# Column sums for the shift and scale vectors of a two-block kernel: transposes with a sum on VectorE, or matmuls with a column of ones

## The chip, the cores and the metric

One core of a Trainium2 chip runs the whole program in one launch. The metric is the device time of an execution in microseconds (us). TensorE (PE) multiplies, VectorE (DVE) and ScalarE (ACT) work on its outputs, GpSimd (POOL) has a small part, and SyncE (SP) issues the transfers.

## What is computed

Two stacks of transformer-like blocks over 256 tokens of width 1024, all in float32. Each of the twelve sublayers normalises its input and shifts and scales it by vectors that come from a conditioning vector:

```python
mod = cond @ ada_w[l] + ada_b[l]                  # 1024 -> 9 * 1024
sh1, sc1, g1, sh2, sc2, g2, sh3, sc3, g3 = jnp.split(mod, N_MOD, axis=-1)
h = modulate(x, norm_ffn1[l], sh1, sc1)           # rms_norm(x, gain) * (1 + scale) + shift
x = x + 0.5 * (1.0 + g1)[:, None] * swiglu(h, ffn1_w1[l], ffn1_w3[l], ffn1_w2[l])
```

The sublayers are feed-forward networks, two mixers with a gated delta rule and latent attention, one state-space mixer, and one pooling mixer. Two sublayers of the second stack also run over a second sequence, with a conditioning vector of its own. What the change touches is `cond @ ada_w` for the shift and scale vectors alone.

## The kernel before, in words

Weights stream through a ring of seven 128x1024 tiles (`raw`). ACT rounds each to a short form (`hi`, L354), DVE takes the rest (`lo`, L355), and TensorE multiplies three times (L360 to L362); some layers multiply whole float32 tiles instead (L386, L412). Outputs of these products stand in the PSUM tag `mm`, four tiles; all other TensorE outputs stand in the tag `ps`, four tiles of 128x512.

The modulation vectors are made in the background, a step at a time between the units of weights (`tick`). `Mods.sums` takes one vector of 1024: for each of eight blocks of 128 input features it loads a 128x1024 piece of `ada_w` into a ring of two tiles (`ad`), and adds it, scaled by the conditioning value of its partition, to a tile `acc` (one buffer): ACT starts it (L537), DVE adds the seven others (L541). Where two conditioning vectors are served, the second has two 128x512 tiles (`pg`) of its own. Then the 128 partitions of `acc` have to be summed.

For gates this sum is wanted as a row on every partition, and `rows` multiplies by a 128x128 block of ones (L559). For shift and scale it is wanted as eight columns of 128, feature by partition, and `cols` (L546) makes it: for each half of `acc`, four 128x128 transposes by TensorE into a `ps` tile (`T4`, L248), and one sum along the free axis by DVE (L551) of 128x512 to 128x4; then the bias is added (L552). `scale` multiplies by the gain afterwards (L586). Ten sublayers take shift and scale this way, two of them for two conditioning vectors, so `cols` runs 24 times; the first sublayer has its own path (`early`), and the pooling mixer uses `rows`.

The order on each engine is not written by hand: a planner orders the instructions at build time by their place in the program, by free tiles and by its own costs; only the weights' loads, `hi` and `lo` are held in sequence (`in_order`). Each engine then runs its list in that order.

A sum by a column of ones is already in use elsewhere, for the norms of queries and keys (L1065): a 128x128 block is the weight, one column of ones moves, and one column of PSUM is written, 16 times in each of four passes through that code.

Of the kernel before, what the change touches and what calls it, by code (L numbers as in the profile page):

```python
# [14 lines left out]
ALU = mybir.AluOpType  # L15
AX = mybir.AxisListType
# [7 lines left out]
KD = D // P  # L24
# [51 lines left out]
def block_kernel(ctx, tc, A, out, stop=None, skip=()):  # L76
    nc = tc.nc
    V, G, T = nc.vector, nc.gpsimd, nc.tensor
# [27 lines left out]
    def nm(s):  # L106
        names[0] += 1
        return f"{s}_{names[0]}"

    def ps():  # L110
        return psp.tile([P, 512], F32, tag="ps", name=nm("ps"))
# [7 lines left out]
    def small(n, dt=F32, tag="sm", bufs=None):  # L119
        return smp.tile([P, n], dt, tag=f"{tag}{n}", name=nm(tag), **({"bufs": bufs} if bufs else {}))  # L120
# [8 lines left out]
    def C(n):  # L129
        a, w = CI[n]  # L130
        return con[:, a:a + w]

    ident, ones = C("ident"), C("ones")
# [39 lines left out]
    gain, adab = {}, {}  # L173
# [24 lines left out]
    def h4(ap):  # L198
        return ap.rearrange("p (h d) -> p h d", d=P)
# [12 lines left out]
    SL = [slice(h * P, (h + 1) * P) for h in range(4)]  # L212
# [33 lines left out]
    def T4(o, src):  # L246
        for sl in SL[0:src.shape[1] // P]:
            T.transpose(o[:, sl], src[:, sl], ident)  # L248
# [256 lines left out]
    class Mods:  # L505
# [38 lines left out]
            yield  # L544

        def cols(self, i, v, tag):  # L546
            o = small(KD, tag=tag, bufs=8)
            for h in range(2):
                q = ps()
                T4(q, self.acc[i][h])  # L550
                V.tensor_reduce(out=o[:, h * 4:h * 4 + 4], in_=h4(q), op=ALU.add, axis=AX.X)  # L551
            V.tensor_add(o, o, adab[self.b, self.l][:, v * KD:(v + 1) * KD])  # L552
            return o

        def rows(self, i, o, mul, add):
# [1564 lines left out]
```

## Time and profile before

| | |
|---|---|
| median of 3 runs | 3086.33 us (3085.15 to 3090.08) |
| the profiled execution, its own time | 3087.46 us |
| its span, first to last instruction | 3085.7 us |
| busy: PE, DVE, ACT, POOL | 2950.2, 2214.3, 1339.0, 162.1 us |
| mean granted TensorE clock | 0.98 |
| moved from and to memory | 606 MB read, 4 MB written |

Busy times are sums over the span, and they are averages over stages with different limits. A stretch of the span has to be read by itself: which engine has no gap in it, and which wait ends last there. The granted clock is given as a share of 2.4 GHz; it has two levels, 1.00 and 0.50. Matmuls overlap, so the mean duration of one is longer than the distance from one to the next; what a group occupies is read from the chain of waits, which gives each piece the time that passed in it. The weight loads (PEld) run beside the matmuls.

### The profile page before, as it was taken

The numbers are of one execution on the slowest core, as the hardware profiler recorded it, in microseconds if no ns is written. First come the engines' busy times: TensorE is split into PE (matmuls) and PEld (weight loads), VectorE is DVE, ScalarE is ACT, GpSimd is POOL, SyncE is SP. The second block draws the span as 40 slices with busy tenths as digits, with TensorE's granted clock in tenths as the row PEclk, the third lists the DMA queues.
The fourth block names the chain that finished last, engine by engine and source line by source line (L and its number), as shares of the span: only waits on it lengthen the run. The fifth ranks groups of instructions, "written<-read, shape, count | busy, mean of one in ns | idle before, by whom it ended". The sixth has DMA issues, their size and how long they took to land.

```text
span 3085.7 us, 44006 instructions
## 1 busy us (share of the span) xinstructions
PE 2950.2 (96%) x16707; PEld 2444.7 (79%) x16707; DVE 2214.3 (72%) x3980; ACT 1339.0 (43%) x2096; POOL 162.1 (5%) x148
## 2 busy tenths in 40 slices
PE   7999999999998999999999999999989999999898
PEld 4988889875575898978876589899865799897697
DVE  6799988665388657887665385675789976878754
ACT  4554454322244445443322354544544644443443
POOL 1000000100002000000100000000043000001000
PEclk9999999999999999999999999999999999999899
DMA  8788886323464857894223475686534487788563
GB/s 280 251 287 292 259 296 208 89 73 106 153 203 170 264 185 229 290 318 131 81 78 109 139 245 183 197 295 194 172 89 130 145 284 233 232 292 296 157 185 129
DMA packets 288921, 613.25 MB, mean 199 GB/s; under 512 B 29480, under 2 KB 75702, under 8 KB 288709
## 3 DMA queue, kind: packets, MB, share of 16 engines
q1 hardware_dynamic: 288709, 610.44, 61.0%
q8 instruction: 131, 2.15, 0.3%
q14 instruction: 81, 0.66, 0.1%
HBM read 606.16 MB, written 4.20 MB: 198 GB/s over the span
## 4 chain that ended last, share of the span: by engine, by line
PE 68%; DVE 17%; DMA 8%; issue 4%; ACT 3%; POOL 1%; SPq 0%; DVEq 0%; ACTq 0%; POOLq 0%
PE mm L360 16%; PE mm L361 15%; PE mm L362 15%; PE mm L386 9%; DMA ad<-ada_w 6%; PE mm L412 4%; DVE acc L541 3%; PE ps L248 2%; DVE lo L355 2%; DVE pg L541 1%; PE ps L1172 1%; PE ps L1165 1%; PE ps L559 1%; DVE pg L1519 1%; DVE pg L1522 1%
## 5 line engine op out<-in xcount | busy, mean ns | idle before, releaser
L354 ACT CAST hi<-raw 128x1024 fp32r<-128x1024 f32 (+1 forms) x587 | 611.1, 1044 | 790.9 <-PE mm L361 308.0
L355 DVE TENSOR_TENSOR lo<-raw,hi 128x1024 fp32r<-128x1024 f32 (+1 forms) x587 | 709.0, 1218 | 293.8 <-ACT hi L354 280.9
L360 PE MATMUL mm<-hTh,lo 128*128 128x256 f32 x2448 | 702.1, 287 | 20.6 <-DVE lo L355 11.7
L361 PE MATMUL mm<-hTh,hi 128*128 128x256 f32 x2448 | 694.4, 284 | 0.0
L362 PE MATMUL mm<-hTl,hi 128*128 128x256 f32 x2448 | 693.9, 284 | 0.1
L360 PEld LDWEIGHTS mm<-hTh,lo 128*128 128x128 f32 x2448 | 470.2, 192 | 27.9 <-DVE lo L355 9.0
L361 PEld LDWEIGHTS mm<-hTh,hi 128*128 128x128 f32 x2448 | 470.7, 192 | 2.3 <-issue 1.2
L362 PEld LDWEIGHTS mm<-hTl,hi 128*128 128x128 f32 x2448 | 470.4, 192 | 0.3 <-DVE hTl L726 0.3
L541 DVE SCALAR_TENSOR_TENSOR acc<-ad,cond,acc 128x1024 f32<-128x1024 f32 x238 | 305.2, 1282 | 82.0 <-DMA ad<-ada_w 80.1
L360 PE MATMUL mm<-hi,pg 128*128 128x512 f32 (+1 forms) x716 | 281.1, 393 | 0.0
L361 PE MATMUL mm<-hi,pg 128*128 128x512 f32 (+1 forms) x716 | 277.5, 388 | 0.0
L362 PE MATMUL mm<-lo,pg 128*128 128x512 f32 (+1 forms) x716 | 275.6, 389 | 0.9 <-DVE lo L355 0.9
L386 PE MATMUL mm<-raw,hTw 128*128 128x512 f32 x448 | 212.1, 604 | 0.0
L412 PE MATMUL mm<-hTw,raw 128*128 128x256 f32 x896 | 204.5, 382 | 1.3 <-ACT pg L1514 1.3
L360 PE MATMUL mm<-hi,hTl 128*128 128x512 f32 (+1 forms) x424 | 174.1, 411 | 22.9 <-DVE hTl L726 14.5
L412 PEld LDWEIGHTS mm<-hTw,raw 128*128 128x128 f32 x896 | 168.7, 191 | 28.5 <-issue 5.0
L386 PE MATMUL mm<-raw,pg 128*128 128x512 f32 (+1 forms) x416 | 179.0, 574 | 1.2 <-ACT pg L1180 1.2
L361 PE MATMUL mm<-hi,hTh 128*128 128x512 f32 (+1 forms) x424 | 167.1, 395 | 0.0
L362 PE MATMUL mm<-lo,hTh 128*128 128x512 f32 (+1 forms) x424 | 166.7, 394 | 0.4 <-DVE lo L355 0.4
L362 PEld LDWEIGHTS mm<-lo,pg 128*128 128x128 f32 x716 | 134.4, 188 | 29.3 <-DVE lo L355 1.6
L360 PEld LDWEIGHTS mm<-hi,pg 128*128 128x128 f32 x716 | 134.7, 188 | 28.6 <-issue 2.0
L361 PEld LDWEIGHTS mm<-hi,pg 128*128 128x128 f32 x716 | 134.7, 188 | 27.7 <-issue 1.0
(433 smaller groups left out, 4355.8 us busy)
## 6 DMA issues: line engine op xcount, KB each, us to landing
ad<-ada_w SPq DMA_DIRECT2D x272, 512.0 KB
raw<-ffn_w SPq DMA_DIRECT2D x264, 512.0 KB
raw<-ffn_w_gate SPq DMA_DIRECT2D x110, 512.0 KB
raw<-ffn_w_up SPq DMA_DIRECT2D x110, 512.0 KB
raw<-ffn_w_down SPq DMA_DIRECT2D x110, 512.0 KB
raw<-w_in SPq DMA_DIRECT2D x104, 512.0 KB
raw<-ssd_w_in SPq DMA_DIRECT2D x60, 512.0 KB
raw<-w_branch_a SPq DMA_DIRECT2D x16, 512.0 KB
```

The costliest lines, as they stand in the source:

```text
L248: T.transpose(o[:, sl], src[:, sl], ident)
L354: in_order("hi", ACT.copy(hi[:, 0:m], raw[:, 0:m]))
L355: in_order(lane, eng.tensor_sub(lo[:, 0:m], raw[:, 0:m], hi[:, 0:m]))
L360: T.matmul(o, sl, mh, start=first, stop=False)
L361: T.matmul(o, sh, mh, start=False, stop=False)
L362: T.matmul(o, sh, ml, start=False, stop=last)
L386: T.matmul(d[c0 // 512][:, 0:min(cw, c0 + 512) - c0], sf, wt[c0 // 512], start=k == 0, stop=k == kt - 1)
L412: T.matmul(acc[m][:, 0:S], wt[0][:, SL[m]], hT.whole[:, k, :], start=k == 0, stop=k == KD - 1)
L541: after_edge(V.scalar_tensor_tensor(out=o, in0=w, scalar=sc, in1=o, op0=ALU.mult, op1=ALU.add))
L559: T.matmul(q, ones, self.acc[i][h], start=True, stop=True)
L1165: T.matmul(blk(y[:, H2[h]]), M[t][:, sl], odd(Ub[t][:, sl]), start=True, stop=True)
L1172: T.matmul(z[:, H2[h]], Tb[t][:, sl], Y[t][:, H2[h]], start=True, stop=True)
```

## The change

For the eight columns there are now eight matmuls. Each takes one 128x128 block of `acc` as its weight and one column of ones as its moving operand, and writes one column of a single `ps` tile. The bias is added straight from that tile. The two DVE sums, the second `ps` tile and the transposes are gone. Nothing else is edited.

```diff
         def cols(self, i, v, tag):
-            o = small(KD, tag=tag, bufs=8)
-            for h in range(2):
-                q = ps()
-                T4(q, self.acc[i][h])
-                V.tensor_reduce(out=o[:, h * 4:h * 4 + 4], in_=h4(q), op=ALU.add, axis=AX.X)
-            V.tensor_add(o, o, adab[self.b, self.l][:, v * KD:(v + 1) * KD])
+            o, q = small(KD, tag=tag, bufs=8), ps()
+            for k in range(KD):
+                T.matmul(q[:, k:k + 1], self.acc[i][k // 4][:, SL[k % 4]], ones[:, 0:1], start=True, stop=True)
+            V.tensor_add(o, q[:, 0:KD], adab[self.b, self.l][:, v * KD:(v + 1) * KD])
             return o
```

## Rows read from the trace of the kernel before

**Rows 1.** The page, busy time of each engine over the span.
```profile
PE 2950.2 (96%) x16707; PEld 2444.7 (79%) x16707; DVE 2214.3 (72%) x3980; ACT 1339.0 (43%) x2096; POOL 162.1 (5%) x148
```
**Rows 2.** TensorE's order of time, L248 on `acc`: start, us, count, idle before.
```profile
158.23 1.09 PE L248 MATMUL ps<-con,acc 128*128 128x128 f32 x8 [0.75 <-DVE acc L541]
...
2829.95 1.09 PE L248 MATMUL ps<-con,acc 128*128 128x128 f32 x8 [0.69 <-DVE acc L541]
```
**Rows 3.** Stretches: length, busy PE, PEld, DVE, ACT, POOL (records), clock, DMA, GB/s.
```profile
160.00:180.00 20.00, 16.63 (x124) 16.24 (x123) 19.65 (x28) 7.72 (x9) 0.00 (x0) 0.91 0.76 248
180.00:200.00 20.00, 17.29 (x117) 15.34 (x116) 19.27 (x26) 9.02 (x13) 0.00 (x0) 1.00 0.83 277
...
300.00:320.00 20.00, 15.89 (x122) 14.99 (x121) 20.00 (x25) 7.32 (x10) 0.00 (x0) 0.97 0.82 253
```
**Rows 4.** The same view around two of the later bursts.
```profile
1240.00:1260.00 20.00, 20.00 (x171) 20.00 (x170) 14.75 (x19) 10.84 (x16) 0.00 (x0) 1.00 0.86 300
...
2040.00:2060.00 20.00, 20.00 (x171) 20.00 (x170) 15.15 (x20) 10.34 (x15) 0.00 (x0) 1.00 0.80 276
```
**Rows 5.** Chain of waits: start, us, piece, instructions merged; a transpose burst, then L1065.
```profile
2047.40 0.87 PE ps L248 x8
```
**Rows 6.** Chain of waits over the whole span: one burst at L1065.
```profile
547.15 1.68 PE ps L1065 x16
```
**Rows 7.** Groups by form: records | busy us, mean ns | idle before.
```profile
L248 PE MATMUL ps<-con,acc 128*128 128x128 f32 x160 | 21.4, 274 | 4.7 <-DVE acc L541 4.7
...
L1065 PE MATMUL ps<-con,pg 128*128 128x1 f32 x128 | 17.7, 264 | 0.0
...
L1065 PEld LDWEIGHTS ps<-con,pg 128*128 128x128 f32 x128 | 18.9, 222 | 1.5 <-ACT pg L1061 0.5 <-issue 0.5
```
**Rows 8.** Groups by form on DVE.
```profile
L551 DVE TENSOR_REDUCE msh<-ps 128x4 f32<-128x512 f32 x24 | 15.6, 685 | 4.4 <-PE ps L248 4.4
...
L552 DVE TENSOR_TENSOR msh<-msh,adab 128x8 f32<-128x8 f32 x12 | 1.9, 162 | 0.0
```
**Rows 9.** Line L646, an addition that reads PSUM: ns min/median/max, first and last start.
```profile
L646 DVE TENSOR_TENSOR esc<-ps,adab x4: 149/150/151, 19.9 to 50.4; 128x2 f32<-128x2 f32 x4
```
**Rows 10.** Chain of waits, 195 to 237 us.
```profile
197.56 1.79 DVE msc L551 x3
...
199.43 0.60 DVE msc L551
...
228.77 1.20 DVE msh L551 x2
...
234.80 5.96 DMA ad<-ada_w
```
**Rows 11.** Chain of waits, 322 to 338 us.
```profile
334.66 1.00 PE ps L248 x9
...
335.69 1.16 ACT acc L537
...
336.87 5.16 DMA ad<-ada_w
```
**Rows 12.** TensorE's order of time, waits that DVE ends, 360 and 974 us.
```profile
360.11 0.55 PE L360 MATMUL mm<-hTh,lo 128*128 128x256 f32 x1 [3.49 <-DVE lo L355]
...
973.96 1.78 PE L1631 MATMUL ps<-pg,pg 128*128 128x512 f32 x2 [3.37 <-DVE msh L551]
```
**Rows 13.** TensorE's order of time, narrow matmuls from 590 us.
```profile
590.88 1.84 PE L1065 MATMUL ps<-con,pg 128*128 128x1 f32 x16
592.59 1.98 PE L1165 MATMUL ps<-pg,pg 128*128 128x64 f32 x16
```
**Rows 14.** Stretches as in Rows 3, around L1065 at 547 and 590 us.
```profile
547.50:548.00 0.50, 0.50 (x6) 0.50 (x7) 0.00 (x0) 0.00 (x0) 0.00 (x0) 1.00 0.00 0
...
596.00:597.00 1.00, 1.00 (x6) 1.00 (x6) 0.00 (x0) 0.99 (x2) 0.00 (x0) 0.50 0.00 0
...
605.00:606.00 1.00, 1.00 (x6) 0.76 (x5) 0.58 (x2) 0.45 (x1) 0.62 (x1) 0.70 0.00 0
```

## The prediction, made before the changed kernel was run

> **What bounds the kernel now.** First the page: TensorE is busy 96% of the span, VectorE 72% [rows 1]. That speaks against adding work to TensorE, but it is an average, so I looked up where the edited work lies. The order of time shows it as twenty bursts of L248 on `acc`, at 158, 192, 227, 252, 325, 364, 438, 471, 967, 1025, 1249, 1281, 1345, 1368, 2047, 2080, 2514, 2547, 2807 and 2830 us [rows 2]; those at 158, 192, 325 and 364 serve two conditioning vectors, which makes 24 calls. Then the stretches around them. Later on TensorE has no gap: 20.00 of 20 us, with DVE busy 15 [rows 4]. Between 150 and 365 us it is otherwise: DVE is busy 19.3 to 20.0 us of 20 and TensorE only 15.9 to 17.3 where it waits [rows 3]. So half the calls lie where TensorE sets the pace, and some where DVE does. Last the chain of waits, for what stands in it at the bursts: the transposes themselves at 2047 [rows 5], the sums L551 at 197 and 229 us [rows 10].
>
> **What a call costs TensorE.** Removed: eight transposes, one record each (160 records for the 20 calls whose source is `acc`) [rows 7]. In the chain a burst occupies 0.87 us [rows 5], or 109 ns a transpose; the mean of 274 ns [rows 7] overlaps its neighbours. Added: eight float32 matmuls with one moving column. The trace of before has this very shape at L1065: 128x128 weight, 128x1 moving. Its 64 calls left 128 records [rows 7], two passes each, so a call of `cols` now gives sixteen. Sixteen such passes took 1.68 us in the chain [rows 6], 105 ns each; the load of a new weight for each pass takes 222 ns beside them [rows 7] and is probably why a single column is no quicker than 128. The difference is 1.68 - 0.87 = 0.81 us a call, 24 x 0.81 = 19.4 us if all of it were on the path.
> The Trainium skill has a rule that would turn this round. "TensorE: Matmul & The Clock Gate", section "Back-to-back issue gap", gives some 60 cycles for 1 to 64 moving columns, about 25 ns; by that sixteen passes would take 0.4 us, less than the transposes, and the sum below would become a gain. The same page's section on LDWEIGHTS gives 128 columns some 107 ns, and the 105 ns at L1065 agree with that one. I take the row.
>
> **What a call saves VectorE.** Removed: two sums at 685 ns [rows 8]; back to back the second follows after 0.60 us in the chain [rows 10], so 1.20 to 1.37 us. The addition L552 stays at 0.16 us [rows 8], but reads PSUM; an addition from PSUM took 0.15 us [rows 9], so I add nothing. 24 x 1.20 = 28.8 us less on DVE, more than TensorE gains in work. What it is worth is decided by place. The order of DVE's list is otherwise kept: the addition now waits for all sixteen passes, where the first sum waited for four transposes, and behind it stand `lo` and L541. Sixteen passes and one addition end 1.68 + 0.16 us after the start, the old way 0.87 + 1.2 + 0.16 at best; so nobody behind it waits longer. One `ps` tile of the four is taken instead of two. `acc` is released by the last pass, 0.81 us later, and ACT's L537 and the `ada_w` load behind it wait for that [rows 11].
>
> **The sum by place.**
> Nine calls where TensorE has no gap (1025, 1249, 1281, 1345, 2047, 2080, 2514, 2547, 2807), as in [rows 4]: DVE's saving falls into its own slack, TensorE's addition goes through, 9 x 0.81 = +7.3 us.
> The calls at 1368 and 2830: TensorE has waited for L541 before them [rows 2], so part of the lateness may go into that wait; half, +0.8 (0 to +1.6).
> The calls at 438 and 471, TensorE again nearly gapless: +1.6 (0 to +1.6).
> The four at 325 and 364: the passes are on TensorE's path, +3.2, but a wait of 3.49 us for `lo` follows at 360 [rows 12] and takes in the first pair; +1.6. From below: that wait hangs on an `ada_w` load of 5.16 us, started when the last transpose had released `acc` [rows 11]. Were the passes put in a better place by the planner, this load could start earlier; -5 to +3.2.
> The six at 158, 192, 227 and 252: DVE has hardly a gap. 3.6 us of L551 stand in the chain (1.79 + 0.60 + 1.20) [rows 10], but the chain goes on through an `ada_w` load of 5.96 us [rows 10], which comes no sooner if the transfers are what it waits for. TensorE pays up to 6 x 0.81 = 4.9 here, of which its waits hide most. I take -2; bounds -7.2 (six calls' sums in full) and +4.9.
> The call at 967: TensorE waits 3.37 us at L1631 until a sum L551 has given a `ps` tile back [rows 12]. With one tile taken instead of two that wait shrinks; -1 (-3.4 to +0.8).
> Together 7.3 + 0.8 + 1.6 + 1.6 - 2 - 1 = +8.3 us. The profiled execution took 3087.46 us and lies 1.1 above the median of 3086.33; so 3095.8 for that execution and 3094.6 for a median.
>
> **The rivals.**
> A. VectorE's relief decides, and the kernel is faster. Place: 150 to 365 us, and 967. Price: the low ends, -7.2 - 5 - 3.4 = -15.6, against 7.3 + 0 + 0 where TensorE is gapless: -8.3, 3078. It wins once the early part gives more than 9.7 us. For it: DVE without a gap [rows 3]. Against: the loads that stand in the chain between the sums [rows 10].
> B. It is absorbed. Waits further on take in half of TensorE's lateness: 7.3 / 2 + 0.8 + 1.6 + 0 - 2 - 1 = +3, 3089. For it: such waits as the one at 360 [rows 12]. Against: most waits behind a gapless stretch wait for that stretch's own result.
> C. The clock falls. With narrow passes from 590.88 us on and no idle before them [rows 13], the granted clock was 0.50 (1.2 GHz) at 596 and came back at 605 [rows 14]; after one burst of sixteen within wide matmuls at 547 it stayed at 1.00 (2.4 GHz) [rows 14]. A call for one vector is like the burst at 547; the four doubled calls, 32 passes of 3.4 us, are like the beginning at 590. If the clock is halved for as long as such a burst lasts, each loses 1.7 us, 6.8 in all; at worst, as at 596, half of 10 us each. With 6.8: 3101.
> D. Narrow passes are cheap, so that TensorE pays nothing: what is left is -2 - 1 and the 3.6 us of chain at most, some 3083. The section on the issue gap named above would have it so; L1065 speaks against it.
>
> **How the numbers follow.** Forecast 45%, A 16%, B 24%, C 11%, D 4%. Not in these prices is what the planner does with changed costs: each engine's order may move, in either direction, and that widens each case by a few us. The range goes from near A, 3079, to beyond C, 3104. A measurement of this kernel tells some 0.2% from no change, 6.2 us: 3080.2 to 3092.5 is the same. Slower by more: nearly all of C and five sixths of the forecast, 10 + 38 = 48%. Faster by more: most of A and a part of D, 16%. The same: 36%.
>
> **What would show it.** On TensorE the bursts become sixteen records of 128x1 and take some 1.7 us in the chain; if they take under 1 us, the cost is wrong and D holds. DVE's busy time falls by about 30 us and L551 is gone; PE's records grow by 192. Around 1240 to 1300 and 2040 to 2100 us everything after a burst should come 0.8 us later for each; if it doesn't, B holds. The first 480 us should take about as long as before; if they are shorter by 6 us or more, A holds. A granted clock under 1.00 right behind one of the four doubled bursts would be C. The forecast would be wrong altogether if the planner's order differs much, in other lines than these, most of all in the order of `ada_w` loads against weights.

## The result

The changed kernel took 3104.23 us at the median (3098.89 to 3115.01) beside 3085.92 (3080.84 to 3094.93) for the kernel before: +18.3 us, ratio 1.0060 with a 95% interval of 1.0037 to 1.0083. Measured once more (`e5_again`) it was 1.0041 (1.0026 to 1.0057), some +13 us. The forecast was slower, 3094.6, in a range up to 3104, and the first median lies just above that range. The direction held; +8.3 is less than half of the first measurement and two thirds of the second.

The profiled execution took 3110.42 us, its span is 3108.6. On the page this line answers to [rows 1]:

```profile
PE 2980.7 (96%) x16899; PEld 2474.0 (80%) x16899; DVE 2190.4 (70%) x3932; ACT 1339.1 (43%) x2096; POOL 163.2 (5%) x148
```

Among the groups by form (records | busy us, mean ns | idle before it) these answer to [rows 7, 8]; below line 547 the line numbers are two lower than before.

```profile
L549 PE MATMUL ps<-con,acc 128*128 128x1 f32 x320 | 37.7, 247 | 2.5 <-DVE acc L541 2.5
L549 PE MATMUL ps<-con,pg 128*128 128x1 f32 x64 | 10.6, 295 | 0.0
...
L549 PEld LDWEIGHTS ps<-con,acc 128*128 128x128 f32 x320 | 38.6, 194 | 4.2 <-DVE acc L541 2.3 <-issue 1.2
...
L550 DVE TENSOR_TENSOR msc<-ps,adab 128x8 f32<-128x8 f32 x12 | 2.0, 165 | 11.2 <-PE ps L549 11.2
L550 DVE TENSOR_TENSOR msh<-ps,adab 128x8 f32<-128x8 f32 x12 | 2.0, 164 | 15.6 <-PE ps L549 15.6
```

The change does what it says: 192 PE records more, 384 passes with one moving column, no sum on DVE, and the addition from PSUM costs 0.16 us as taken. DVE's busy time fell by 23.9 us on the page, where about 30 were forecast. Two things are new. DVE waits 26.8 us in front of L550, where it waited 5.8 in front of the sums (4.4 for `msh` [rows 8], and 1.4 for `msc`). And the mean of a pass is 247 ns where its weight is `acc`, but 295 where it is `pg`, which happens only at the second half of a doubled burst.

What a burst takes in the chain of waits is as forecast (start, us, piece), to be held against [rows 5]:

```profile
2063.16 1.68 PE ps L549 x16
```

The stretches around the calls at 2047 and 2080, now at 2063 and 2097 (length, busy PE, PEld, DVE, ACT, POOL, clock, DMA, GB/s), are as gapless as in [rows 4], with less work on DVE:

```profile
2060.00:2080.00 20.00, 19.97 (x168) 19.76 (x167) 13.79 (x17) 9.05 (x11) 0.00 (x0) 1.00 0.73 232
2090.00:2110.00 20.00, 20.00 (x170) 20.00 (x169) 10.90 (x15) 8.38 (x11) 0.00 (x0) 1.00 0.66 212
```

The surprise stands in TensorE's order of time at the doubled bursts, beside a single one:

```profile
160.23 3.27 PE L549 MATMUL ps<-con,pg 128*128 128x1 f32 x16
...
193.04 2.10 PE L549 MATMUL ps<-con,acc 128*128 128x1 f32 x16 [0.76 <-DVE acc L541]
...
195.99 3.41 PE L549 MATMUL ps<-con,pg 128*128 128x1 f32 x16
...
2062.99 1.84 PE L549 MATMUL ps<-con,acc 128*128 128x1 f32 x16
```

The same sixteen passes take nearly twice as long as the second half of a doubled burst. Stretches of one us there show why: the clock is at 0.50. At 194 us it falls before the first sixteen passes are through.

```profile
160.00:161.00 1.00, 1.00 (x9) 1.00 (x9) 1.00 (x2) 0.00 (x0) 0.00 (x0) 0.78 0.54 152
...
163.00:164.00 1.00, 1.00 (x6) 1.00 (x6) 0.46 (x2) 0.95 (x2) 0.00 (x0) 0.50 0.75 247
166.00:167.00 1.00, 1.00 (x7) 1.00 (x6) 1.00 (x1) 0.00 (x0) 0.00 (x0) 0.50 0.99 363
...
194.00:195.00 1.00, 1.00 (x10) 1.00 (x10) 1.00 (x2) 0.00 (x0) 0.00 (x0) 0.84 0.92 344
...
199.00:200.00 1.00, 1.00 (x4) 0.90 (x5) 0.56 (x3) 0.39 (x2) 0.00 (x0) 0.50 0.68 186
203.00:204.00 1.00, 1.00 (x4) 0.81 (x3) 1.00 (x3) 0.00 (x0) 0.00 (x0) 0.50 0.83 227
```

To see where the time went I took the wide matmuls (L360 to L362, L386, L412), which are the same 13736 in every kernel, counted them, and compared when the one with the same number starts. The table has the time between two of them, named by their start in the kernel before, and the time at the lower clock between 140 and 500 us. Where TensorE sets the pace, half of that time is lost.

| profile | 140 to 500 | of it at clock 0.50 | 500 to 1000 | 2000 to 2120 (two calls) | 2500 to 2600 (two calls) |
|---|---|---|---|---|---|
| before | 360.0 | 10.2 | 500.2 | 120.2 | 99.3 |
| before, second profile (`e9_before`) | 363.9 | 13.6 | 498.0 | 120.2 | 99.3 |
| changed | 373.2 | 30.6 | 498.4 | 123.1 | 101.4 |
| changed, second profile (`e5_again`) | 368.7 | 20.4 | 501.2 | 122.1 | 101.7 |
| `e1_single` | 367.3 | 17.0 | 493.6 | 123.1 | 101.2 |
| `e2_double`, `e12_double_again` | 368.9, 372.4 | 34.0, 27.2 | 496.8, 495.0 | 120.2, 120.2 | 99.4, 99.3 |
| `e10_double_wide`, `e11_wide_again` | 360.1, 360.8 | 13.6, 6.8 | 494.5, 495.1 | 120.2, 120.2 | 99.3, 99.3 |
| `e3_no_sum` | 361.0 | 17.0 | 496.0 | 121.5 | 100.0 |
| `e6_wide` | 366.1 | 10.2 | 500.5 | 123.0 | 102.8 |
| `e8_acc2` | 372.8 | 27.2 | 492.5 | 124.9 | 102.6 |
| `e4_spread` | 372.0 | 34.0 | 500.4 | 122.6 | 102.1 |
| `e7_twice` | 407.0 | 64.7 | 496.0 | 128.6 | 107.7 |

So from 140 to 500 us the changed kernel loses 9 to 13 us (5 to 9 beside the second profile of the kernel before), where the forecast had +1.2. Eight of the nine gapless calls can be read in the same way, in the stretches from 1020 to 1100, 1230 to 1320, 2000 to 2120, 2500 to 2600 and 2780 to 2826 us: they cost 9.7 and 7.7 us in the two profiles, 1.0 to 1.2 each. Around the call at 2830, from 2826 to 2900 us, 7.2 and 2.9 us are lost; in the first profile the clock fell there too, with 13.6 us more at 0.50 than in the kernel before. Two profiles of one kernel differ as well, those of the kernel before by 7.4 us from 1000 to 2000.

### The profile page after: what moved, and what is told of

It is laid out like the page before. It is cut to its first block, busy times and chain, and to the rows that moved or that the text cites. A ratio compares the mean times of both kernels' runs of the same rounds, so it can differ in the third digit from the quotient of the medians.

```text
span 3108.6 us, 44334 instructions
## 1 busy us (share of the span) xinstructions
PE 2980.7 (96%) x16899; PEld 2474.0 (80%) x16899; DVE 2190.4 (70%) x3932; ACT 1339.1 (43%) x2096; POOL 163.2 (5%) x148
## 4 chain that ended last, share of the span: by engine, by line
PE 70%; DVE 17%; DMA 6%; ACT 3%; issue 3%; POOL 0%; SPq 0%; DVEq 0%; ACTq 0%; POOLq 0%
PE mm L360 16%; PE mm L362 16%; PE mm L361 15%; PE mm L386 9%; PE mm L412 4%; DMA ad<-ada_w 4%; DVE acc L541 2%; DVE lo L355 2%; PE ps L248 2%; PE ps L549 1%; DMA raw<-ffn_w 1%; PE ps L1163 1%; PE ps L1170 1%; DVE pg L541 1%; PE ps L557 1%
## 5 line engine op out<-in xcount | busy, mean ns | idle before, releaser
L360 PE MATMUL mm<-hTh,lo 128*128 128x256 f32 x2448 | 703.4, 288 | 15.8 <-DVE lo L355 7.8
L362 PE MATMUL mm<-hTl,hi 128*128 128x256 f32 x2448 | 695.2, 284 | 0.1
L360 PEld LDWEIGHTS mm<-hTh,lo 128*128 128x128 f32 x2448 | 471.9, 193 | 23.2 <-DVE lo L355 8.3
L362 PEld LDWEIGHTS mm<-hTl,hi 128*128 128x128 f32 x2448 | 471.7, 193 | 0.3 <-DVE hTl L724 0.3
L360 PE MATMUL mm<-hi,pg 128*128 128x512 f32 (+1 forms) x716 | 283.5, 396 | 0.1
L362 PE MATMUL mm<-lo,pg 128*128 128x512 f32 (+1 forms) x716 | 280.1, 392 | 0.0
L386 PE MATMUL mm<-raw,hTw 128*128 128x512 f32 x448 | 212.1, 604 | 0.0
L412 PE MATMUL mm<-hTw,raw 128*128 128x256 f32 x896 | 204.9, 382 | 3.9 <-ACT pg L1512 3.9
L412 PEld LDWEIGHTS mm<-hTw,raw 128*128 128x128 f32 x896 | 168.7, 191 | 31.1 <-issue 5.5
L360 PE MATMUL mm<-hi,hTl 128*128 128x512 f32 (+1 forms) x424 | 173.6, 409 | 19.9 <-DVE hTl L724 12.5
L386 PE MATMUL mm<-raw,pg 128*128 128x512 f32 (+1 forms) x416 | 178.8, 574 | 1.2 <-ACT pg L1178 1.2
L362 PE MATMUL mm<-lo,hTh 128*128 128x512 f32 (+1 forms) x424 | 166.8, 395 | 0.0
L360 PEld LDWEIGHTS mm<-hi,pg 128*128 128x128 f32 x716 | 136.3, 190 | 29.6 <-issue 2.0
L362 PEld LDWEIGHTS mm<-lo,pg 128*128 128x128 f32 x716 | 136.2, 190 | 28.6 <-issue 0.5
```

The source lines that it names most:

```text
L360: T.matmul(o, sl, mh, start=first, stop=False)
L362: T.matmul(o, sh, ml, start=False, stop=last)
L386: T.matmul(d[c0 // 512][:, 0:min(cw, c0 + 512) - c0], sf, wt[c0 // 512], start=k == 0, stop=k == kt - 1)
L412: T.matmul(acc[m][:, 0:S], wt[0][:, SL[m]], hT.whole[:, k, :], start=k == 0, stop=k == KD - 1)
```

## The experiments

My theory after the result, T: TensorE pays for the passes wherever it has no gap, the clock falls behind the doubled bursts, and DVE's relief brings little. Rivals: A, the relief counts; P, the planner's changed order of loads makes the first 500 us late; R, the later release of `acc` does; B, waits take the passes in.

**Single calls alone.** `cols` chooses by the number of conditioning vectors; with one it makes the eight matmuls, with two the transposes and sums:

```diff
+            if len(self.conds) == 1:
+                o, q = small(KD, tag=tag, bufs=8), ps()
+                for k in range(KD):
+                    T.matmul(q[:, k:k + 1], self.acc[i][k // 4][:, SL[k % 4]], ones[:, 0:1], start=True, stop=True)
+                V.tensor_add(o, q[:, 0:KD], adab[self.b, self.l][:, v * KD:(v + 1) * KD])
+                return o
+            else:
+                o = small(KD, tag=tag, bufs=8)
+                for h in range(2):
...
```

> Only the 16 calls for one conditioning vector are changed; the 8 calls at the doubled bursts keep transposes and sums. Theory T (TensorE pays some 0.9 us a call where it has no gap, and the clock falls behind the doubled bursts; the relief of DVE is worth next to nothing): 11 calls x 0.9 us and the part of four early single calls that isn't hidden, +8 to +12 us on the kernel before, no fall of the granted clock in the first 480 us that the kernel before hasn't. Rival A (DVE's relief counts): 0 or faster. Rival P (the lateness of the first 480 us comes from a changed order of loads, whatever the form of the sums): the first 480 us late by 5 us or more here too.

Measured: ratio 1.0017 (1.0004 to 1.0030), +5 us, under what T expected, and no fall of the clock right behind the bursts at 158 and 192. The two calls in the gapless stretch cost 2.9 us. From 140 to 500 us it lost 7.3 (3.4 beside the second profile of before), so this run doesn't exclude P. From 500 to 1000 it gained 6.6 (4.4), with only the call at 967 there: profiles move by some us in places where no call lies, which limits what one profile can tell.

**Doubled bursts alone.** The same with the condition turned round:

```diff
-            if len(self.conds) == 1:
+            if len(self.conds) > 1:
```

> Only the 8 calls that make up the four doubled bursts (two conditioning vectors) are changed. Theory T: the granted clock is 0.50 right behind each of the four bursts and the first 480 us get 6 to 11 us longer; from 480 us on as in the kernel before, so +6 to +11 us in all. Rival A: these calls lie where DVE has hardly a gap, so 3 to 8 us faster. Rival P: late without a fall of the clock.

Measured: 1.0007 (0.9994 to 1.0020), and on another chip 1.0010 (0.9996 to 1.0025). The clock fell behind each of the four bursts as expected and from 140 to 500 us it is late by 9 and 12 us, but the whole is only 2 to 3 us later than the kernel before, under the +6 to +11 of T: from 500 to 1000 us 3 to 5 us come back.

**The relief of DVE alone.**

```diff
                 T4(q, self.acc[i][h])
-                V.tensor_reduce(out=o[:, h * 4:h * 4 + 4], in_=h4(q), op=ALU.add, axis=AX.X)
-            V.tensor_add(o, o, adab[self.b, self.l][:, v * KD:(v + 1) * KD])
+                V.tensor_add(o[:, h * 4:h * 4 + 4], h4(q)[:, :, 0], adab[self.b, self.l][:, v * KD + h * 4:v * KD + h * 4 + 4])
```

> The transposes of the kernel before stay; the two sums on DVE are left out (an addition of one column of each transposed block stands for them, so the sum over partitions is not computed). It shows what DVE's relief alone is worth, with TensorE's work as before. Theory T: nothing that can be told from no change, 0 to -3 us. Rival A: -8 to -16 us, in the first 480 us.

Measured: 1.0000 (0.9986 to 1.0013), 140 to 500 us in 361.0. DVE's busy time fell by 27.5 us, and that is worth nothing that can be told (-4 to +4 us), with TensorE's work as it was. Rival A, -8 us or more, is out in this form.

**Passes apart.**

```diff
-                self.out["sh"] = [self.cols(i, v, "msh") for i in range(len(self.conds))]
+                o = []
+                for i in range(len(self.conds)):
+                    if i:
+                        yield
+                    o.append(self.cols(i, v, "msh"))
+                self.out["sh"] = o
...
```

The same stands in `scale`.

> The whole change, but at a doubled burst the sums of the second conditioning vector come one step of the background work later, so that wide matmuls stand between the two bursts of sixteen passes. Theory T with the clock as a part of its own: no fall of the clock behind these bursts, 4 to 8 us less than the changed kernel, that is +9 to +14 us on the kernel before. If the falls have nothing to do with the length of the burst, it is as slow as the changed kernel, +17 to +20 us.

Measured: 1.0038 (1.0023 to 1.0054). The edit missed its aim: the planner put the second sixteen passes directly behind the first all the same at 159, 333 and 374 us and with 0.4 us between them at 206, and the clock fell as before. It decides nothing.

**The change once more,** with no edit.

> The changed kernel as it is, on the chip of the three runs beside it, since single executions of one kernel lie up to 20 us apart. If its lateness is one of form (theory T), +12 to +20 us on the kernel before; if a good part of the first measurement was spread, +6 to +10, the sum of the two halves tried apart.

Measured: 1.0041 (1.0026 to 1.0057), 3103.69 beside 3092.65 at the medians. The intervals of the two measurements overlap, from 1.0037 to 1.0057: 11 to 18 us. This second one lies at the lower end of what T expected.

**128 columns instead of one.** Against the kernel before:

```diff
             for h in range(2):
                 q = ps()
-                T4(q, self.acc[i][h])
-                V.tensor_reduce(out=o[:, h * 4:h * 4 + 4], in_=h4(q), op=ALU.add, axis=AX.X)
-            V.tensor_add(o, o, adab[self.b, self.l][:, v * KD:(v + 1) * KD])
+                for sl in SL:
+                    T.matmul(q[:, sl], self.acc[i][h][:, sl], ones, start=True, stop=True)
+                V.tensor_add(o[:, h * 4:h * 4 + 4], h4(q)[:, :, 0], adab[self.b, self.l][:, v * KD + h * 4:v * KD + h * 4 + 4])
```

> The changed kernel with all 128 columns of ones moving instead of one (into two tiles, of which one column in 128 is read): as many passes and weight loads, no sums on DVE, but the array moves 128 columns in each pass. Theory T, clock part: the granted clock stays at 1.00 behind the doubled bursts, and the first 480 us get 4 to 8 us shorter than with one column; a pass costs at most some 5 ns more, 24 x 16 x 0.005 = 2 us. So +8 to +14 us on the kernel before. If the clock falls all the same, it is as late as the changed kernel.

Measured: 1.0052 (1.0033 to 1.0070). Behind the doubled bursts the clock stayed at 1.00, and from 140 to 500 us it was 2.6 to 7.1 us shorter than the changed kernel, as T has it; but the whole, +12 to +16 us, was no faster, and at the upper end of T's +8 to +14 or above. What it loses after 500 us lies at the gapless calls: the eight that the table's method can read cost 11.9 us, where they cost 9.7 and 7.7 in the changed kernel. Why more, the runs don't show; it has two tiles and two additions for each call, where the changed kernel has one.

**Passes twice.** Each of the eight matmuls is made two times.

```diff
-            for k in range(KD):
+            for k in [k for k in range(KD) for _ in range(2)]:
```

> The changed kernel with each of the eight matmuls made twice, 32 passes a call instead of 16. Theory T, pass part: 16 x 0.106 = 1.7 us more for each call where TensorE has no gap, at least the eleven from 1025 us on, so +19 us on the changed kernel and more where the clock falls behind these longer bursts too: +19 to +35. If waits take the lateness in (rival B), half of that or less.

Measured: 1.0279 (1.0253 to 1.0304), 3179.90 beside 3103.69 of `e5_again` on the same chip, +76 us, twice the upper end. Passes explain 24 x 1.7 = 41 us of it at most. For the rest there is the clock: by the mean granted clock of its executions 107 us of full clock are lost, 63 in `e5_again`, so 44 more. Now single calls have it too. The burst at 2105 us, 32 passes, in TensorE's order of time:

```profile
2105.25 4.41 PE L549 MATMUL ps<-con,acc 128*128 128x1 f32 x32
```

And the stretches around it, in columns as in [rows 3]:

```profile
2106.00:2107.00 1.00, 1.00 (x11) 1.00 (x10) 0.00 (x0) 0.49 (x1) 0.00 (x0) 1.00 0.70 106
2109.00:2110.00 1.00, 1.00 (x6) 1.00 (x6) 0.30 (x2) 0.30 (x1) 0.00 (x0) 0.50 0.00 0
2112.00:2113.00 1.00, 1.00 (x7) 1.00 (x6) 0.20 (x1) 0.00 (x0) 0.00 (x0) 0.50 0.75 184
```

No wait takes such a burst in; rival B, half of the expected lateness or less, is out for this size.

**Two buffers for `acc`.** A page is given up for it.

```diff
-    pgp = ctx.enter_context(tc.tile_pool(name="pgp", bufs=39))
+    pgp = ctx.enter_context(tc.tile_pool(name="pgp", bufs=38))
...
-    acp = ctx.enter_context(tc.tile_pool(name="acp", bufs=1))
+    acp = ctx.enter_context(tc.tile_pool(name="acp", bufs=2))
```

> The changed kernel with two buffers for the tile acc, so that the next vector doesn't wait until the sixteen passes have released it (one of the 39 pages is given up for the room). Theory T: no faster than the changed kernel by more than 3 us. Rival R (the later release holds up the loads of ada_w, and these the first 480 us): 5 to 10 us faster than the changed kernel, with the first 480 us as in the kernel before.

Measured: 1.0056 (1.0035 to 1.0078), 372.8 us from 140 to 500. R is out.

**The kernel before, a second profile.**

> The kernel before once more, unchanged, for a second profile: how far two profiles of one kernel lie apart from 140 to 500 us and from 500 us to the end. Theory T needs less than 5 us in each, since the two profiles of the changed kernel show 9 and 13 us more in the first and 8 and 11 us in the second.

Measured: 3.9 us more from 140 to 500, 3 us from there to the end, under 5 as T needs, though not by much. The 7.4 us from 1000 to 2000 named above are in the 3, less some 4 the other way round in other stretches.

**Doubled bursts with 128 columns.** Transposes and sums for the single calls, and for the doubled ones the matmuls of `e6_wide`, followed by a copy of one column in 128 and the addition as before. Against the kernel before:

```diff
                 q = ps()
+                if len(self.conds) > 1:
+                    for sl in SL:
+                        T.matmul(q[:, sl], self.acc[i][h][:, sl], ones, start=True, stop=True)
+                    V.tensor_copy(o[:, h * 4:h * 4 + 4], h4(q)[:, :, 0])
+                    continue
                 T4(q, self.acc[i][h])
```

> Only the four doubled bursts are changed, to sixteen passes a vector with 128 moving columns of ones, no sums on DVE; all other calls keep transposes and sums. Beside the run that changed the same bursts with one moving column. Theory T: no fall of the clock right behind these bursts; 140 to 500 us late by 2 to 5 us (8 x 0.9 us of passes less what waits take in) instead of 9; +2 to +5 us in all. If the clock falls all the same, late by 8 us or more from 140 to 500 us.

Measured: 0.9986 (0.9973 to 0.9998), faster than expected; 360.1 us from 140 to 500 and no fall of the clock right behind the bursts. So it was made again, beside the same bursts with one column on the same chip.

> The four doubled bursts with 128 moving columns, all else as before, measured again and on the same chip as the next run. Theory T with DVE's relief counted at these bursts: 2 to 6 us faster than the kernel before, no fall of the clock right behind the bursts. If the earlier gain was spread: no change that can be told.

> The same four bursts with one moving column. Theory T: the clock falls behind each of the four, and it is 4 to 9 us slower than the run beside it with 128 columns; against the kernel before 0 to +5 us. If the number of moving columns has no part in it: no slower than the run beside it by more than 2 us.

Measured: 0.9976 (0.9962 to 0.9991), 3083.84 us, with 128 columns; 1.0010 (0.9996 to 1.0025), 3094.19 us, with one. TensorE's order of time with one column:

```profile
335.14 1.84 PE L550 MATMUL ps<-con,acc 128*128 128x1 f32 x16
336.85 1.93 PE L550 MATMUL ps<-con,pg 128*128 128x1 f32 x16
```

The stretches behind it, and the one from 140 to 500 us:

```profile
338.00:340.00 2.00, 2.00 (x18) 2.00 (x19) 1.30 (x4) 0.17 (x1) 0.00 (x0) 0.95 1.04 296
340.00:342.00 2.00, 2.00 (x11) 2.00 (x11) 2.00 (x3) 0.00 (x0) 0.00 (x0) 0.50 0.94 353
...
140.00:500.00 360.00, 340.39 (x2196) 310.29 (x2195) 315.36 (x429) 162.14 (x221) 0.00 (x0) 0.96 0.82 275
```

The order of time with 128 columns, at the same burst:

```profile
332.77 1.06 PE L552 MATMUL ps<-con,acc 128*128 128x128 f32 x8
333.66 1.95 PE L552 MATMUL ps<-con,pg 128*128 128x128 f32 x16
```

And its stretches, the same in length:

```profile
336.00:338.00 2.00, 2.00 (x19) 2.00 (x18) 0.90 (x3) 0.00 (x0) 0.00 (x0) 1.00 0.86 256
338.00:340.00 2.00, 2.00 (x19) 2.00 (x18) 0.03 (x1) 1.05 (x1) 0.00 (x0) 1.00 0.88 334
...
140.00:500.00 360.00, 342.95 (x2271) 312.09 (x2271) 325.54 (x489) 167.02 (x229) 0.00 (x0) 0.99 0.84 282
```

The first burst shows the two with the same wait ahead and the same sixteen passes on `acc` behind it. One column:

```profile
160.69 2.12 PE L550 MATMUL ps<-con,acc 128*128 128x1 f32 x16 [0.78 <-DVE acc L541]
...
162.00:164.00 2.00, 2.00 (x13) 2.00 (x12) 2.00 (x2) 0.26 (x1) 0.00 (x0) 0.58 0.59 150
```

128 columns:

```profile
157.05 2.05 PE L552 MATMUL ps<-con,acc 128*128 128x128 f32 x16 [0.74 <-DVE acc L541]
158.94 0.83 PE L552 MATMUL ps<-con,pg 128*128 128x128 f32 x6
...
158.00:160.00 2.00, 2.00 (x19) 2.00 (x19) 2.00 (x3) 0.00 (x0) 0.00 (x0) 1.00 0.69 186
```

With as many passes, the kernel with one column is 10 us slower at the median and 11.6 from 140 to 500 us in the profiles; in that stretch 27.2 us at 0.50 stand against 6.8, which is 10.2 us of full clock. What is left for the order of the loads (P) is small. The gain of the wide bursts came out a little larger than T's 2 to 6 us, and so did the distance between the two runs, for which T had 4 to 9. It is not quite one variable: the planner, too, places the wider passes otherwise (16 and 6 together, ten later at 157 us; eight and then 24 together at 323 and 361 us), and the copies wait for them 0.7 us in all where the additions wait 3.4. But 24 passes with 128 columns in one piece left the clock at 1.00.

## Why the prediction was right in direction and short in size

**What bounds the kernel** held: TensorE is as busy as before, and less work on DVE is worth nothing that can be told by itself (`e3_no_sum`).

**The price of a call** held. 1.68 us of chain a burst and 0.81 more than the transposes were taken from L1065 and came out to the digit. Rival D fell with it. By the table in the Trainium skill, "TensorE: Matmul & The Clock Gate", section "Back-to-back issue gap", some 25 ns a pass, a burst would have taken 0.4 us, as an estimate; the trace differs and decides. The section gives that table for a matmul by itself and says that in a stream of weight loads and matmuls both set the spacing, which the prediction left out. The step from the wide matmul ahead of a burst to the one behind it grew a little more than the chain says, 0.9 us, from 0.91 to 1.83 at 2047 and at 2080 us. That the column count is not what a pass costs shows `e6_wide`: at the median 112 ns lie between the starts of two passes, with 128 moving columns there as with one in the changed kernel.

**Nine calls where TensorE has no gap, +7.3.** Two of them, from 2000 to 2120 us, cost 2.9 and 1.9 us in the two profiles; in the first, part of it is a new wait of 0.5 us for DVE ahead of the first call. Over the eight that can be read it is 1.0 to 1.2 us each instead of 0.81, so this term was of the right size and a little short. Waits further on gave nothing back that can be told, so rival B is not seen here: from 2120 to 2440 us, without a call, the changed kernel takes 316.1 and 317.6 us and the kernel before 319.9 and 318.0, and the one that stands out had 17.1 us there at 0.50, the changed kernel 10.2 in both.

**The call at 2830, +0.4:** 7.2 and 2.9 us were lost around it. Shortly ahead of the burst TensorE waits for DVE, 2.8 us in all in both profiles, 1.3 in the kernel before. In the first the clock fell within the sixteen passes, and 6.8 of the 7.2 us are the clock.

**The six and the four calls from 158 to 364, -2 and +1.6.** This is the step that failed: at the doubled bursts the sum had nothing for the clock, against relief and waits that took the passes in. From 140 to 500 us the kernel is 13.2 and 8.7 us later, where the forecast had +1.2 with the two calls behind them. 10.2 and 5.1 us of that are the clock: 30.6 and 20.4 us at 0.50 where the kernel before had 10.2, half of the difference (its second profile had 13.6, which leaves 8.5 and 3.4). Rival C had the place, the bursts and a price of 6.8; I gave it 11% of the chances and put nothing of it into the sum, though [rows 13, 14] showed a fall with no idle before it. That its price came out so near is luck in part: it took the clock to be down for as long as the burst lasts, and it was down for 3 to 10 us each time. The relief that I had set against it didn't come.

**The clock over whole executions.** Each execution on record has its mean granted clock. What this lacks to 1.00, times the span, is the most that the lower clock can have cost; where TensorE waits for others it cost less. The means, each beside the kernel before on the same chip, in us:

| kernel | executions | lost to the clock, against before | time, against before |
|---|---|---|---|
| changed (`e5_again`) | 12 | +5.6 | +12.7 |
| `e1_single` | 12 | +1.3 | +5.0 |
| `e2_double`, `e12_double_again` | 12, 12 | +8.8, +7.7 | +2.7, +2.7 |
| `e10_double_wide`, `e11_wide_again` | 12, 12 | -3.6, -4.9 | -4.9, -7.3 |
| `e6_wide` | 7 | -4.1 | +13.9 |
| `e7_twice` | 5 | +49.6 | +84.2 |

The standard error of a loss is some 2 us, 3 to 4 in the last two lines. So in the changed kernel the clock is at most about 6 us of the 13, and the rest is near the +8.3 of the forecast. The clock is not needed for a kernel to be late: `e6_wide` lost no more to it than the kernel before and was as late as the changed kernel. Between `e11_wide_again` and `e12_double_again` it is the clock: 12.5 us lost, for 10 us of time.

**Where DVE's 29 us went.** I had written that nobody behind the addition waits longer. The waits before L550 show otherwise: the planner puts the addition close behind the passes, and DVE, which works in order, stands still for it 19 times, 26.8 us in all. At the first doubled burst, DVE's order of time:

```profile
161.88 0.16 DVE L550 TENSOR_TENSOR msh<-ps,adab 128x8 f32<-128x8 f32 x1
163.54 0.17 DVE L550 TENSOR_TENSOR msh<-ps,adab 128x8 f32<-128x8 f32 x1 [1.49 <-PE ps L549]
163.62 2.35 DVE L355 TENSOR_TENSOR lo<-raw,hi 128x1024 fp32r<-128x1024 f32 x2
```

The `lo` behind it could have run: the load that it waits for had landed at 161.5 us. So part of DVE's busy time turned into waiting time on DVE. But only 5.7 us of the 26.8 stand before 400 us, where DVE has hardly a gap and the sums of ten calls took 13.7; later on DVE has slack, and such a wait costs nothing by itself. What became of the rest of the early relief isn't shown.

**The calls at 967, -1, at 1345 and at 1368:** not settled; profiles of one kernel differ there by as much.

**What stays open.** The two halves of the change measure +5 and +2 to +3, the whole +11 to +18; the intervals just allow that it is a sum. The doubled half loses 8 us to the clock and only 3 of time, so at these bursts either something was won or part of the clock's loss fell into waits; the runs don't tell which. And why 128 columns at the doubled bursts beat the kernel before: from 140 to 500 us they are no faster than it (360.1 and 360.8 beside 360.0 and 363.9). The gain lies behind that, from 500 to 1000 us, where `e1_single`, `e2_double` and `e3_no_sum`, and `e8_acc2` and `e7_twice` with the whole edit, gain as much beside its first profile. By the whole executions most of the gain goes along with the clock, to which these two kernels lost 3.6 and 4.9 us less. Why the clock stood higher there is open.

## What to carry to other kernels

Price a narrow matmul by its passes, not by its columns: in float32 a one-column product of a 128x128 block took twice the time of that block's transpose (1.68 us for eight, against 0.87), and taking the sums off VectorE paid nothing that could be told. Behind runs of narrow matmuls TensorE's clock was found at half with little or no idle time ahead, and what followed paid for it; where the trace of before shows such a fall, give it a term in the sum and not only a rival. And an operation that is short on its engine can still hold it for as long as what it waits for.

## What the runs showed of the hardware

Sixteen passes with one moving column (1.7 us) within wide matmuls left the granted clock at 1.00 at the gapless single calls of both profiles of the changed kernel. At each of the four doubled bursts, in both, 32 passes were followed or cut by a clock of 0.50 (1.2 GHz). Three of these are 32 in one piece; at 193 us wide matmuls stand between the two sixteens, and the clock fell within the first of them, behind a wait of 0.8 and 1.1 us. With 128 moving columns 24 passes in one piece (2.8 us) left it at 1.00 in `e6_wide`, `e10_double_wide` and `e11_wide_again`, and so did 22 behind a wait of 0.74 us. In the 10 us ahead of the eight falls TensorE was idle for 0 to 1.8 us, and not at all ahead of the one at 338 us in the first profile. The Trainium skill, "TensorE: Matmul & The Clock Gate", section "Why this matters for your kernels", names idle gaps between bursts as what lowers the clock; these traces show that it also falls without one. Two single calls behind waits have a fall within them or 1 us behind too, in the first profile: at 1383 us, with 1.5 us of waits ahead, and at 2849, with 2.8. In `e7_twice`, with 32 passes a call, twelve of the sixteen single calls showed a fall within them or up to 1.3 us behind them, the other four none.
